# A GEGLU MLP on one core: w_down sums moved into the first pair of the following quad, and the owed gelu flushed one product later

## The chip, the cores and the metric

One core of a Trainium2 chip. The metric is the device time of one execution in microseconds (us), the median of several; all runs quoted here are fast, with a granted TensorE clock of 0.999 or 1.0. PE is TensorE, DVE VectorE, ACT ScalarE, POOL GpSimd, and SP the engine from which most transfers are issued.

## The reference

```python
x: (8, 1024, 1024) f32;  w_gate, w_up: (1024, 4096) f32;  w_down: (4096, 1024) f32
gate = x @ w_gate
up   = x @ w_up
gate = 0.5 * gate * (1 + tanh(sqrt(2 / pi) * (gate + 0.044715 * gate ** 3)))
return ((gate * up) @ w_down).astype(float32)
```

## The kernel before

The 8192 tokens are worked off in eight passes of 1024. Matrix products are made with fast (Strassen-like) schemes in f16: fewer matmuls, in exchange for sums of operands and results on DVE and ACT. Passes 0 to 2 use a scheme of 7 products instead of 8; in the gate/up stage of such a pass, one *pair* of column blocks of the weights takes 14 products (seven for gate, seven for up), and one product is four matmuls of 128x128 by 512. Two pairs are a *quad*: they share one load of raw weights.

Four names matter in a pair: P1 writes bank a, P5 bank b, then P6 adds onto bank a. Since P1's own result is needed later, ACT copies bank a to bank c ("copy 0" for gate, "copy 1" for up) before P6 may overwrite it.

```python
SEQ = [
    ("P1", 0), ("P1", 1), ("P5", 0), ("P6", 0), ("P6", 1), ("P5", 1), ("P7", 0),
    ("P7", 1), ("P2", 0), ("P4", 0), ("P4", 1), ("P2", 1), ("P3", 0), ("P3", 1),
]
AFTER1 = {                       # work put behind product k
    1: ["copy 0"], 2: ["copy 1"], 4: ["snap s2 0"], 5: ["snap s2 1"],
    ...
    13: ["add s2 0"], 14: ["add s2 1"],
}

def pair(p, i, extra, seq, after):
    ...
    for k, (name, w) in enumerate(seq, 1):
        product(name, w)
        if k == 1:
            flush()                          # gelu and product owed by the pair before
        for what in after.get(k, ()):
            do(what)                         # copy, snap: ACT; add, h: DVE
        for f in extra.get(k, ()):
            f()
    pending.extend([lambda: do("gelu s2"), lambda: do("prod s2")])
```

The last sums of a pair, "add s2" on DVE, end after its last product, so the gelu on them (ACT) and the product of gate and up (POOL) are owed to the next pair: `flush()` issues them there. The other names in `AFTER1`: a "snap" is ACT's copy of a finished bank to a tile in SBUF, an "add" is DVE's sum of bank b and such a tile, and an "h" is DVE's product of gate and up. ACT works through its own stream in the order in which the program issues it: in the lines of the prediction two copies whose input was ready stand behind a gelu before which ACT had been idle for 4.44 us.

In pass 0 the kernel also prepares w_down for the later down stages: in four groups it loads raw blocks of w_down (line 394, POOL's DMA queue, with a cast), makes four sums of them on DVE (lines 410, 412, 414, 416) and stores the results. `s0 + ds` is a running product number; 14 of them are a pair.

```python
for n in range(4):
    s0 = 28 * n + 59
    for ds, f, a in (
        (0, wd_load, (n, 0)), (2, wd_load, (n, 1)),
        (4, wd_load, (n, 2)), (6, wd_load, (n, 3)),
        (18, wd_sums, (0,)), (19, wd_sums, (1,)),
        (20, wd_sums, (2,)), (21, wd_sums, (3,)), (23, wd_store, (n,)),
    ):
        pr, k = divmod(s0 + ds - 1, 14)
        if pr == i:
            at(k + 1, f, *a)
```

In the first down stage, the transposing loads of x for the next pass and the loads of the stage's own w_down operands (chunks) share SP's queue:

```python
for v, name in enumerate(DSEQ):              # 7 products of 2 chunks kc each
    for nb in range(2):
        kc = 2 * v + nb
        for g in range(G):
            ... # 8 matmuls
            if nb == 0 and g == 0 and p + 1 < NPASS:
                ...
                if v == (3 - p if p < FAST - 1 else 0):
                    transpose_x(p + 1)       # four transposing DMAs
        load_d(p, kc + 6 if p else {0: 8, 6: 10, 8: 12}.get(kc, 14))
```

## Time and profile before

| | us |
|---|---|
| median of the first three runs | 2263.22 (2263.08 to 2264.55) |
| median of six runs | 2263.05 (2262.39 to 2264.55) |
| span of the profiled execution | 2261.1 |
| PE busy, PE idle by the page | 2247.4, 13.7 |
| gate/up stage of pass 0, 1, 2 | 183.75, 195.99, 194.86 |
| down stage of pass 0, 1, 2 | 97.69, 96.69, 96.70 |
| from the end of pass 2 to the end | 1366.9 |

The stages are differences of the first matmul starts of the stages in PE's timeline. The views and how to read them are shown with the prediction; the one thing to keep in mind is that a matmul's printed duration, 0.379 us, is not its share of time: in an unbroken run one starts every 0.216 us, as the prediction works out.

### The profile page before, as it was taken

Reading aid. Unit: us, or ns where it says so; the run is one execution under the profiler, and the core shown is the slowest. Engines: PE = TensorE matmul, PEld = TensorE weight load, DVE = VectorE, ACT = ScalarE, POOL = GpSimd, SP = SyncE. Lnnn points to the kernel's source line nnn. Section 1 sums busy time; section 2 is a strip of 40 time slices with the busy share of each in tenths; the row PEclk is TensorE's granted clock in tenths of the full one; section 3 lists DMA queues with packets and bytes.
Section 4 is the critical chain, followed back from the end, with each engine's and each line's share of the span. In section 5 each row is a group of like instructions: output and inputs, shape, how many; then the busy total and the mean of one; then the engine's idle time right before and its main releaser. Section 6 shows DMA issues by size and latency. Waiting matters only on the chain.

```text
span 2261.1 us, 42805 instructions
## 1 busy us (share of the span) xinstructions
PE 2247.4 (99%) x16634; PEld 1624.9 (72%) x16634; DVE 1565.3 (69%) x2190; ACT 954.6 (42%) x1866; POOL 686.0 (30%) x825
## 2 busy tenths in 40 slices
PE   9999999999999999999999999999999999999999
PEld 4444444444444445888888888888888888888888
DVE  6676468884488755877776677766776667866674
ACT  4444135651266522665126550355404553055520
POOL 1342013330133300555115450245402543044520
PEclk9999999999999999999999999999999999999999
DMA  9997969989999999999998999988999889888876
GB/s 241 191 207 187 274 189 236 253 258 284 266 223 243 270 311 346 332 336 379 302 336 275 318 301 317 326 273 321 310 320 318 282 313 325 312 314 277 283 288 225
DMA packets 308093, 642.46 MB, mean 284 GB/s; under 512 B 79088, under 2 KB 185328, under 8 KB 287344
## 3 DMA queue, kind: packets, MB, share of 16 engines
q1 hardware_dynamic: 253104, 566.57, 73.0%
q0 software_dynamic: 54784, 73.14, 19.2%
q8 instruction: 130, 2.13, 0.4%
q14 instruction: 75, 0.61, 0.1%
HBM read 574.36 MB, written 138.41 MB: 315 GB/s over the span
## 4 chain that ended last, share of the span: by engine, by line
PE 84%; DVE 3%; DMA 2%; SPq 0%; issue 0%; ACT 0%; DVEq 0%
PE ps L848 40%; PE ps L1099 20%; PE ps L626 14%; PE ps L991 10%; DMA wd_quads<-x_sums 1%; DVE ring L351 1%; DVE h_s L278 1%; DVE tmp L645 1%; DMA w_ops<-h_s 1%; SPq L255 0%; DMA ring<-wd_ops 0%; DVE x_sums L278 0%; DVE h_a L663 0%; ACT ps L642 0%; DVE h_a L923 0%
## 5 line engine op out<-in xcount | busy, mean ns | idle before, releaser
L848 PEld LDWEIGHTS <-ring 128*128 128x128 f16 x8320 | 814.1, 98 | 94.4
L825 POOL TENSOR_TENSOR h_a<-tmp 128x256 f16<-128x256 f32 x640 | 468.8, 752 | 839.8 <-ACT tmp L813 832.3
L848 PE MATMUL ps<-x_sums,ring 128*128 128x256 f16 x5760 | 655.8, 273 | 0.0
L810 DVE TENSOR_TENSOR tmp<-tmp,ps 128x512 f32<-128x512 f32 x640 | 414.4, 683 | 146.9 <-PE ps L848 100.4
L626 PEld LDWEIGHTS <-ring 128*128 128x128 f16 x2632 | 257.4, 98 | 317.0 <-issue 8.2
L795 ACT COPY tmp<-ps 128x512 f32<-128x512 f32 x520 | 304.0, 585 | 237.7 <-PE ps L848 163.9
L626 PE MATMUL ps<-x_sums,ring 128*128 128x512 f16 x1504 | 342.1, 379 | 4.1 <-DVE tmp L645 2.2
L813 ACT ACTIVATE tmp<-tmp 128x256 f32<-128x256 f32 x640 | 263.8, 418 | 173.3 <-DVE tmp L808 79.7
L848 PE MATMUL ps<-x_b,ring 128*128 128x256 f16 x2560 | 305.6, 273 | 0.0
L808 DVE TENSOR_TENSOR tmp<-ps,tmp 128x512 f32<-128x512 f32 x240 | 165.4, 689 | 145.2 <-ACT tmp L795 101.0
L652 POOL TENSOR_TENSOR h_a<-tmp 128x512 f16<-128x512 f32 x94 | 151.6, 1613 | 374.7 <-ACT tmp L650 259.8
L626 PE MATMUL ps<-x_b,ring 128*128 128x512 f16 x1128 | 259.2, 379 | 0.0
L1099 PEld LDWEIGHTS <-h_a 128*128 128x128 f16 x2240 | 219.1, 98 | 25.4
L991 PE MATMUL ps<-ring,h_a 128*128 128x512 f16 x1024 | 222.3, 379 | 0.8 <-DMA ring<-wd_ops 0.8
L1099 PE MATMUL ps<-ring,h_a 128*128 128x256 f16 x1920 | 216.1, 273 | 0.0
L991 PEld LDWEIGHTS <-h_a 128*128 128x128 f16 x1152 | 112.7, 98 | 137.0 <-DMA ring<-wd_ops 1.3
L645 DVE TENSOR_TENSOR tmp<-ps,tmp 128x512 f32<-128x512 f32 x188 | 127.2, 683 | 107.0 <-ACT tmp L637 104.1
L1156 ACT ACTIVATE tmp<-ps 128x512 f32<-128x512 f32 x60 | 35.3, 597 | 362.6 <-PE ps L1099 274.6
L1168 DVE SCALAR_TENSOR_TENSOR tmp<-ps,tmp 128x512 f32<-128x512 f32 x120 | 81.1, 690 | 97.5 <-PE ps L1099 66.7
L637 ACT COPY tmp<-ps 128x512 f32<-128x512 f32 x188 | 110.0, 586 | 87.2 <-PE ps L626 84.4
L351 DVE TENSOR_TENSOR ring<-ring 128x1024 f16<-128x1024 f16 x188 | 133.1, 722 | 8.7 <-DMA ring<-in_w_up_dram 4.5
L1099 PE MATMUL ps<-ring,x_sums 128*128 128x256 f16 x1120 | 126.4, 273 | 0.0
(102 smaller groups left out, 1536.6 us busy)
## 6 DMA issues: line engine op xcount, KB each, us to landing
ring<-w_ops SPq DMA_DIRECT2D x480, 512.0 KB, 4.8
ring<-wd_quads SPq DMA_DIRECT2D x110, 1024.0 KB, 6.8
ring<-wd_ops SPq DMA_DIRECT2D x35, 1024.0 KB, 8.0
out_dram<-tmp SPq DMA_DIRECT2D x128, 256.0 KB, 6.5
w_ops<-h_s SPq DMA_DIRECT2D x128, 256.0 KB, 7.0
ring<-in_w_gate_dram POOLq DMA_DIRECT2D x23, 1024.0 KB, 10.2
ring<-in_w_up_dram POOLq DMA_DIRECT2D x23, 1024.0 KB, 17.9
wd_quads<-x_sums SPq DMA_DIRECT2D x131, 128.0 KB, 6.5
```

The lines of the kernel that those rows point to most:

```text
L351: nc.vector.tensor_tensor(o, a, b, op)
L626: nc.tensor.matmul(ps(b, w), lhs[:, k], rhs[:, k, :], start=(first and k == 0), stop=(k == KH - 1), skip_group_check=True,)
L645: nc.vector.tensor_tensor(o, ps("b", w), o, ADD)
L652: nc.gpsimd.tensor_tensor(hq[TO[n]][:, i, :], tmp[:, t[n, 1]], tmp[:, t[n, 0]], MUL)
L795: nc.scalar.copy(tmp[:, t[o[1]]], ps_all[:, bank[o[2]]])
L808: nc.vector.tensor_tensor(d, b, a, SUB)
L810: nc.vector.tensor_tensor(d, a, b, ADD if o[4] == "add" else SUB)
L813: nc.scalar.activation(d, d, GELU, scale=GSC)
L825: nc.gpsimd.tensor_tensor(h, tmp[:, t[o[1]], MQ : 2 * MQ], g, MUL)
L848: nc.tensor.matmul(ps_all[:, bank[c], w * MQ : (w + 1) * MQ], lhs[:, w, k], rhs[:, k], start=(first and w == 0 and k == 0), stop=(k == KH ...
L991: nc.tensor.matmul(ps_all[:, bank[b, g]], lhs[:, j, g * P : (g + 1) * P], dc[:, n, :], start=(first and j == 0), stop=(j == NP - 1), skip_ ...
L1099: nc.tensor.matmul(ps_all[:, bank[c], m * MQ : (m + 1) * MQ], lhs[:, j, m * P : (m + 1) * P], rhs[:, j, :], start=(first and j == 0 and m ...
```

## The change

Two edits with one intent: to take away what PE waits for in the pairs of passes 0 to 2. The owed work goes behind both copies; the w_down sums leave the pair in which DVE waited for their loads and go into the pair after it, with loads that start 13 products later.

```diff
             product(name, w)
-            if k == 1:
-                flush()
             for what in after.get(k, ()):
                 do(what)
+            if k == 2:
+                flush()
             for f in extra.get(k, ()):
                 f()
 ...
-                    s0 = 28 * n + 59
+                    s0 = 28 * n + 72
                     for ds, f, a in (
                         (0, wd_load, (n, 0)), (2, wd_load, (n, 1)),
                         (4, wd_load, (n, 2)), (6, wd_load, (n, 3)),
-                        (18, wd_sums, (0,)), (19, wd_sums, (1,)),
-                        (20, wd_sums, (2,)), (21, wd_sums, (3,)), (23, wd_store, (n,)),
+                        (22, wd_sums, (0,)), (23, wd_sums, (1,)),
+                        (24, wd_sums, (2,)), (25, wd_sums, (3,)), (26, wd_store, (n,)),
                     ):
```

## The prediction

> **What bounds the kernel now.** I read the page first. Its first section says that there is little to win:
>
> ```profile
> PE 2247.4 (99%) x16634; PEld 1624.9 (72%) x16634; DVE 1565.3 (69%) x2190; ACT 954.6 (42%) x1866; POOL 686.0 (30%) x825
> ```
>
> The reader is to see that TensorE (PE) is busy for 2247.4 of 2261.1 us. Nothing of its own work is changed (the built programs have the same PE instructions in the same order), so only waits can be won: 13.7 us of visible idle time. Next, the waits of PE alone:
>
> ```profile
> PE ps L626 <- DVE tmp L645: 2.2, 7, 0.4
> PE ps L626 <- ACT ps L642: 1.9, 4, 0.5
> ...
> PE ps L991 <- DMA ring<-wd_ops: 0.8, 1, 0.8
> ```
>
> L626 is the matmul of the gate/up pairs in passes 0 to 2, which the change touches: eleven waits, 4.1 us. The other idle time is the start (4.5 us before 30 us), one DMA wait in the first down stage (0.8) and the tail after the last matmul (about 4.3); the sum is 13.7. None of those three is touched. The fast passes after 894 us show no wait.
>
> Where the eleven lie, I took from PE's timeline. One of them, in pass 0:
>
> ```profile
> 86.60 4.48 PE L626 MATMUL ps<-x_b,ring 128*128 128x512 f16 x20
> 90.92 1.03 PE L626 MATMUL ps<-x_sums,ring 128*128 128x512 f16 x4
> 92.34 4.48 PE L626 MATMUL ps<-x_sums,ring 128*128 128x512 f16 x20 [0.40 <-DVE tmp L645]
> ...
> 99.25 4.48 PE L626 MATMUL ps<-x_b,ring 128*128 128x512 f16 x20
> ```
>
> A product is four matmuls. Twenty take 4.48 us, of which the last matmul's own 0.379 us is pipeline, so one starts every (4.48-0.379)/19 = 0.216 us, a product takes 0.863 us and a pair of 14 products 12.08 us. The run of 20 is the last three products of a pair (P2, P3, P3) and the first two of the next (P1, P1), so a pair begins 12 matmuls into it, here at 89.19. Its third product is P5 (90.92); the fourth is P6, on the bank that P1 wrote. P6 should start 4 x 0.216 after 90.92, at 91.78; it starts at 92.34. **The loss is 0.56 us, though the profile calls 0.40 idle**: the printed end of a matmul lies 0.163 us (0.379-0.216) after the point where the next could have started. The starts of the runs agree: 86.60 to 99.25 is 12.65, against 12.08 for a pair without a wait.
>
> Why P6 waits is in the timeline of all engines:
>
> ```profile
> 86.33 1.27 POOL L652 TENSOR_TENSOR h_a<-tmp 128x512 f16<-128x512 f32 x1 [6.93 <-ACT tmp L650]
> 86.37 1.77 DVE L416 TENSOR_TENSOR h_s<-h_s 128x1024 f16<-128x1024 f16 x1
> ...
> 90.46 0.68 DVE L645 TENSOR_TENSOR tmp<-ps,tmp 128x512 f32<-128x512 f32 x1
> ...
> 91.17 0.63 ACT L650 ACTIVATE tmp<-tmp 128x512 f32<-128x512 f32 x1 [4.44 <-DVE tmp L645]
> ...
> 91.71 1.06 ACT L642 COPY ps<-ps 128x512 f32<-128x512 f32 x2
> ```
>
> The add "s2 0" (L645) of the previous pair ends late, at 91.14. The owed gelu (L650) waits for it, and the two copies of the P1 sums (L642) stand behind the gelu on ScalarE though their input was ready at about 91. P6 overwrites the bank that copy 0 reads, so it waits for that copy, which ends near 92.3. The profile names DVE since another add happens to end at 92.34; I take the copy as the releaser, because the program has P6 wait for ScalarE. A wait in pass 1 has the same form, with ScalarE named:
>
> ```profile
> 372.37 0.63 ACT L650 ACTIVATE tmp<-tmp 128x512 f32<-128x512 f32 x1 [4.38 <-DVE tmp L645]
> ...
> 372.90 1.06 ACT L642 COPY ps<-ps 128x512 f32<-128x512 f32 x2
> ...
> 373.53 2.75 PE L626 MATMUL ps<-x_sums,ring 128*128 128x512 f16 x12 [0.34 <-ACT ps L642]
> ```
>
> All eleven waits stand between P5 and P6, four in pass 0 in the pair after the w_down sums, four in pass 1, three in pass 2.
>
> **What the Trainium skill says.** "PSUM — Partial Sum Buffer", section "Engine vs sequencer instructions": the ScalarE, VectorE and GpSimd queues are strict FIFO. The trace agrees: copies whose input was ready stood behind a gelu that sat 4.44 us for an add. "SBUF — State Buffer", section "Who interferes with whom": a VectorE instruction with two SBUF inputs contends with a GpSimd instruction that reads SBUF. The trace agrees: the sum L416 started inside a GpSimd product and took 1.77 us, all four of its kind 1.767 or more, against 0.68 for L412. "DMA: Bandwidth & Descriptors", section "Anatomy of one DMA — SWDGE (gpsimd) path", has a fit of about 2.0 us plus bytes over 436 GB/s, which gives an estimate of 2.6 us for the 256 KB w_down loads; the trace has 9.1 to 12.3 from issue to landing behind other traffic, and I use the trace.
>
> **The change part by part.** *Flush one product later.* The owed gelu and its GpSimd product move behind both copies. Copy 0 then needs only P1's end (pair start + 0.86, some 0.1 to see it), and ends near +1.55; P6 is due at +2.59. Nothing late stands ahead of it, so each of the eleven waits should go. From the starts of the runs as above their costs are: pass 0, 4 x 0.56 = 2.25; pass 1, 0.50+0.69+0.36+0.69 = 2.24; pass 2, 0.35+0.70+0.36 = 1.41. **The sum is 5.9 us.** No instruction is added. What is delayed: the gelu now starts at +2.4 (after copy 1) and ends near +3.0. Next on ScalarE is the snap of s2, which cannot start before P6 ends at about +3.55. So it is free, except where another ScalarE operation of 1.06 us (L374) and one of 0.63 us stand there too: once in pass 2, by my count of the steps, snap would end 0.1 to 0.2 us after P7 wants it at +5.18. I give 0.2 us for this.
>
> *Sums into the next pair.* Their four loads move 13 products (11.2 us) later, the four sums 17 products. The first sum now waits 13.8 us in four waits for its loads, but that is idle time of VectorE at the start of a pair, where its next work comes only at 83.97 anyway; taking it away gives PE nothing directly. Before, the loads went out from 68.67 and VectorE came to the first sum at 78.0, 9.3 us later. Now they should go out some 4.5 us into a pair (behind the later GpSimd product) and the sum come some 9 us into the next: 12.1-4.5+9 = 16.6 us, enough for the longest, 12.3. Removing 0.68x3+1.77 = 3.8 us from one pair's VectorE and putting it into the next one's last five products does not shorten the chain: I reckon with the add s2 0 about 2 us into the following pair, as late as today. With copies ahead of the gelu that no longer matters. So: 0 us beside the flush.
>
> Sum: 2263.2 - 5.9 + 0.2 = 2257.5.
>
> **The rivals.** (1) *Only part goes*: if the sums are what made the adds late, and the order on ScalarE not, then only pass 0's 2.25 us go: 2261.0. Against it: passes 1 and 2 show the same chain without any such sum. (2) *VectorE becomes late enough to matter*: the bank that P5 takes is freed by the h product on VectorE. In the pairs with the moved sums that product should end near +11.5 to +11.8, and P5 is due at +13.8 on the same scale; for a stall the sums would have to come 2 us later than I think. Four such stalls of 0.5 us would leave 2259.5. (3) *A transfer*: weight loads now follow the w_down loads more closely. DMA is nearly full in pass 0 (0.92 to 1.17 busy between 40 and 180 us). But a weight load lands in 8.6 to 15.1 us and is needed some 22 after its issue; a delay of 4 us stays hidden. (4) *The DMA wait in the first down stage* (0.8) could grow or go with shifted traffic: about 1 us either way.
>
> **Range and chances.** The three runs before spread over 1.5 us. With that, rival 4 and half of rival 2: 2255.8 to 2260.2. Two per cent is 45 us, over three times all visible idle time; slower by that needs a fault that I do not see.
>
> **What would show it.** Right: no PE wait at L626 in any of the eleven places; every pair 12.08 us apart; PE's wait list left with the start and the L991 line; L642 ahead of L650 in each pair; no wait of L410 for its load; the add s2 0 still late in the pairs after the sums. Wrong: a PE wait for h (L663) or for the snap (L637), a longer L991 wait, or waits at L626 that survive, which would mean that the copy was not the releaser.

## The result, and the profile after

2256.48 us (median of six, 2255.86 to 2259.28) against 2263.05 (six runs on the same chips). The ratio is 0.9973, with a 95% interval of 0.996 to 0.9986: the mean time of the changed kernel's fast runs over that of the fast runs of before in the same rounds, so not quite the ratio of the medians. By the yardstick of 2% this is the same; the difference of 6.6 us is clear of the spread all the same, since none of these six runs of before is below 2262.39 and none of the changed kernel above 2259.28.

The line of the changed kernel's page that answers to the first one in the prediction:

```profile
PE 2246.1 (100%) x16634; PEld 1625.6 (72%) x16634; DVE 1561.7 (69%) x2190; ACT 956.1 (42%) x1866; POOL 679.3 (30%) x825
```

PE has the same instructions and 1.3 us less busy time in a span of 2254.4 us, 6.7 less: what went is mostly idle time (13.7 us before, 8.3 now). The waits of PE, whole list (what is waited for, us in total, times, longest):

```profile
PE ps L1219 <- DVE h_s L1222: 1.6, 1, 1.6
PE ps L1198 <- DVE x_b L305: 1.1, 2, 0.6
PE ps L1198 <- ACT ring L331: 0.6, 1, 0.6
PE ps L991 <- DMA ring<-wd_ops: 0.4, 1, 0.4
PE ps L303 <- DVE h_a L297: 0.2, 1, 0.2
```

All eleven waits at L626, the matmul of the pairs, are gone. What remains are the start (lines 303, 1198, 1219) and one transfer in the first down stage. PE's timeline over the first 320 us (start, duration, engine, line, operation, output and inputs, shape, count) at the place that the prediction shows:

```profile
86.58 4.48 PE L626 MATMUL ps<-x_b,ring 128*128 128x512 f16 x20
90.90 5.34 PE L626 MATMUL ps<-x_sums,ring 128*128 128x512 f16 x24
...
98.67 4.48 PE L626 MATMUL ps<-x_b,ring 128*128 128x512 f16 x20
```

P5, P6 and P7 are one unbroken run of 24, and the pairs are 98.67-86.58 = 12.09 us apart, where it had been 12.65. All engines at the next start of a pair, which begins twelve matmuls into the run of 98.67, at 101.26; the sums have moved into the pair before it:

```profile
101.59 0.68 DVE L645 TENSOR_TENSOR tmp<-ps,tmp 128x512 f32<-128x512 f32 x1
102.19 0.68 DVE L416 TENSOR_TENSOR h_s<-h_s 128x1024 f16<-128x1024 f16 x1
102.32 0.57 ACT L642 COPY ps<-ps 128x512 f32<-128x512 f32 x1 [3.52 <-PE ps L626]
...
103.24 0.57 ACT L642 COPY ps<-ps 128x512 f32<-128x512 f32 x1 [0.35 <-PE ps L626]
103.72 0.63 ACT L650 ACTIVATE tmp<-tmp 128x512 f32<-128x512 f32 x1
```

Copy 0 starts as soon as P1 is done ("<-PE ps L626": ACT waited for PE, not for DVE) and the gelu comes third. Two things differ from what the prediction says: the add s2 0 ends at 102.27, 1.0 us into the pair and not 2, and L416 takes 0.68 us and not 1.77.

Where the time went, stage by stage (us):

| stage | before | changed | difference |
|---|---|---|---|
| start, to the first L626 | 28.54 | 28.72 | +0.18 |
| gate/up, pass 0 | 183.75 | 181.32 | -2.43 |
| down, pass 0 | 97.69 | 97.29 | -0.40 |
| gate/up, pass 1 | 195.99 | 193.39 | -2.60 |
| gate/up, pass 2 | 194.86 | 193.39 | -1.47 |
| the rest | 1460.3 | 1460.3 | 0.0 |

The rest is both other down stages and the five fast passes. The sum is -6.7, the difference of the spans (2261.1-2254.4). Each column is one profile: the -0.40 is within what the down stage varies by, and in passes 1 and 2 a delay of 0.25 to 0.5 us comes and goes from profile to profile while the gelu is ahead of the copies (see the sums alone). The two stages of 193.39 are 896 matmuls at 0.2158 us each: at that rate nothing is left to win there without fewer matmuls.

### The profile page after: what moved, and what is told of

Read it like the earlier page. It is cut to its first block, busy times and chain, and to the rows that moved or that the text cites. A ratio compares the mean times of both kernels' runs of the same rounds, so it can differ in the third digit from the quotient of the medians.

```text
span 2254.4 us, 42805 instructions
## 1 busy us (share of the span) xinstructions
PE 2246.1 (100%) x16634; PEld 1625.6 (72%) x16634; DVE 1561.7 (69%) x2190; ACT 956.1 (42%) x1866; POOL 679.3 (30%) x825
## 3 DMA queue, kind: packets, MB, share of 16 engines
q0 software_dynamic: 54784, 73.14, 19.3%
## 4 chain that ended last, share of the span: by engine, by line
PE 87%; DMA 2%; SPq 0%; DVE 0%; issue 0%; DVEq 0%
PE ps L848 40%; PE ps L1099 20%; PE ps L626 17%; PE ps L991 10%; DMA wd_quads<-x_sums 1%; SPq L255 0%; DMA ring<-wd_ops 0%; DVE x_sums L452 0%; DVE h_a L923 0%; DVE tmp L1168 0%; DVE x_sums L278 0%; SPq L487 0%; DVEq L278 0%; SPq L535 0%
## 5 line engine op out<-in xcount | busy, mean ns | idle before, releaser
L626 PEld LDWEIGHTS <-ring 128*128 128x128 f16 x2632 | 257.5, 98 | 310.4
L626 PE MATMUL ps<-x_sums,ring 128*128 128x512 f16 x1504 | 339.8, 379 | 0.0
L626 PE MATMUL ps<-x_b,ring 128*128 128x512 f16 x1128 | 259.1, 379 | 0.0
L652 POOL TENSOR_TENSOR h_a<-tmp 128x512 f16<-128x512 f32 x94 | 144.5, 1537 | 374.8 <-ACT tmp L650 271.9
L991 PE MATMUL ps<-ring,h_a 128*128 128x512 f16 x1024 | 222.3, 379 | 0.4 <-DMA ring<-wd_ops 0.4
L991 PEld LDWEIGHTS <-h_a 128*128 128x128 f16 x1152 | 112.7, 98 | 136.6 <-DMA ring<-wd_ops 0.9
L645 DVE TENSOR_TENSOR tmp<-ps,tmp 128x512 f32<-128x512 f32 x188 | 127.2, 683 | 112.6 <-ACT tmp L637 111.1
L351 DVE TENSOR_TENSOR ring<-ring 128x1024 f16<-128x1024 f16 x188 | 138.7, 751 | 11.1 <-DMA ring<-in_w_up_dram 6.9
```

The lines of the kernel that those rows point to most:

```text
L351: nc.vector.tensor_tensor(o, a, b, op)
L626: nc.tensor.matmul(ps(b, w), lhs[:, k], rhs[:, k, :], start=(first and k == 0), stop=(k == KH - 1), skip_group_check=True,)
L645: nc.vector.tensor_tensor(o, ps("b", w), o, ADD)
L652: nc.gpsimd.tensor_tensor(hq[TO[n]][:, i, :], tmp[:, t[n, 1]], tmp[:, t[n, 0]], MUL)
L991: nc.tensor.matmul(ps_all[:, bank[b, g]], lhs[:, j, g * P : (g + 1) * P], dc[:, n, :], start=(first and j == 0), stop=(j == NP - 1), skip_ ...
```

## The experiments

Two theories of why the eleven waits went. The first: P6 waits for copy 0 alone, and copy 0 stood on ACT behind a gelu that waited for a late add; the order on ACT is the whole cause, and the moved sums add nothing. The second: DVE is what is late, and in pass 0 the sums had to move. Each run below was compared with before in five rounds on one chip.

| run | edit to | median us | gate/up 0, 1, 2 | down 0 | waits at L626 |
|---|---|---|---|---|---|
| flush alone | before | 2257.21 | 181.43, 193.39, 193.39 | 98.92 | 0 |
| sums alone | before | 2260.37 | 181.32, 195.49, 195.11 | 97.11 | 6 |
| gelu between the copies | before | 2256.58 | 181.31, 193.46, 193.47 | 97.29 | 0 |
| sums early | before | 2260.85 | 181.32, 195.48, 195.10 | 98.26 | 6 |
| load first | changed | 2255.66 | 181.32, 193.39, 193.38 | 96.69 | 0 |
| changed, again | none | 2256.43 | 181.40, 193.39, 193.39 | 97.46 | 0 |
| flush alone, load first | before | 2255.80 | 181.31, 193.38, 193.38 | 96.70 | 0 |
| load first, again | changed | 2255.85 | 181.31, 193.39, 193.39 | 96.69 | 0 |

Before, in the same rounds: 2262.99 for the first four, 2263.26 for the next two, 2262.60 for the last two. The stages are from the one profiled execution of each. All outputs are right.

### The flush alone

The kernel before with the first hunk of the diff and not the second.

> The kernel before with the flush alone moved behind the second copy; the w_down loads and sums stay where they were. Theory (the copy behind the late gelu is what holds P6; its order on ScalarE is the whole cause): all eleven PE waits at L626 go, PE's three gate/up stages take about 181.3, 193.4 and 193.4 us as in the changed kernel, time 6.0 to 6.7 us below before, within 0.7 us of the changed kernel. VectorE still waits about 13.8 us at L410 and still takes 1.77 us for L416, and the add s2 0 in the pairs of the sums is still about 1.9 us late: none of it costs PE anything. Rival (the moved sums are needed for pass 0): passes 1 and 2 gain 4.1 us, pass 0 nothing, four waits of 0.4 at L626 remain, time about 4.1 us below before.

Measured: 2257.21 us (2256.26 to 2258.30), ratio 0.9973, interval 0.9961 to 0.9986. The timeline of all engines where the prediction shows the wait of before; this pair starts at 87.11 + 12 x 0.216 = 89.70:

```profile
86.84 1.27 POOL L652 TENSOR_TENSOR h_a<-tmp 128x512 f16<-128x512 f32 x1 [4.78 <-ACT tmp L650]
86.89 1.77 DVE L416 TENSOR_TENSOR h_s<-h_s 128x1024 f16<-128x1024 f16 x1
...
90.77 0.57 ACT L642 COPY ps<-ps 128x512 f32<-128x512 f32 x1 [3.52 <-PE ps L626]
90.98 0.68 DVE L645 TENSOR_TENSOR tmp<-ps,tmp 128x512 f32<-128x512 f32 x1
91.43 1.89 PE L626 MATMUL ps<-x_sums,ring 128*128 128x512 f16 x8
...
92.17 0.63 ACT L650 ACTIVATE tmp<-tmp 128x512 f32<-128x512 f32 x1
```

The late DVE is all there: L416 at 1.77 us, the add s2 0 ending at 91.66, 1.96 us into the pair as before (91.14-89.19 = 1.95), and 16.2 us of waiting at L410 for the loads. But copy 0 starts before the add has even begun, and P5 and P6 are one run. All gate/up stages are within 0.12 us of their floor. The second theory falls for the change as made: with the flush moved, the sums need not move. This kernel's median is 0.7 us above the changed kernel's, in other rounds; in the profiled execution, the slowest of the five, most of the excess is in the down stage (98.92 us against 97.29). The last experiment comes back to it.

### The sums alone

The second hunk of the diff and not the first.

> The kernel before with the w_down loads and sums alone moved into the next pair; the owed gelu stays ahead of the copies. The prediction on record had this part at 0 us, with the add s2 0 about 2 us late as before: then four L626 waits of about 0.4 remain in pass 0 and the time is that of before. The theory after seeing the changed trace: there that add ends 1.0 us into the next pair (L416 takes 0.68 us instead of 1.77), so that even with the gelu ahead copy 0 ends at about +2.2 where P6 is due at +2.59: pass 0 loses its four waits (183.75 us becomes 181.3 to 181.6), passes 1 and 2 keep their seven (195.99 and 194.86 us), time about 2.3 us below before.

Measured: 2260.37 us (2259.98 to 2260.91), 2.6 us below before by the medians; ratio 0.9987, interval 0.9975 to 1.0000. The waits of PE at L626 that are left, six and all in passes 1 and 2:

```profile
PE ps L626 <- ACT ps L642: 1.6, 3, 0.5
...
PE ps L626 <- DVE tmp L645: 0.6, 3, 0.2
```

And the timeline of all engines in pass 0, at the pair that starts at 101.76:

```profile
102.10 0.68 DVE L645 TENSOR_TENSOR tmp<-ps,tmp 128x512 f32<-128x512 f32 x1
102.70 0.68 DVE L416 TENSOR_TENSOR h_s<-h_s 128x1024 f16<-128x1024 f16 x1
102.81 0.63 ACT L650 ACTIVATE tmp<-tmp 128x512 f32<-128x512 f32 x1 [3.50 <-DVE tmp L645]
...
103.34 1.06 ACT L642 COPY ps<-ps 128x512 f32<-128x512 f32 x2
```

The gelu still stands ahead of the copies, but the add is done at 102.78, 1.0 us into the pair; copy 0 ends at about 103.9 and P6 is due at 101.76+2.59 = 104.35. So this part alone is worth all of pass 0's 2.43 us. The prediction had it at 0 beside the flush; its working, with the add as late as before, leaves 0 for the part by itself too, and that was wrong. Either part wins pass 0's waits (2.43 us here, 2.32 with the flush alone), and together they win them once.

Seven waits had been expected to stay and six did. The missing one is in pass 1, where the program is that of before: there the add s2 0 of one pair ended 1.89 us into the next pair in the profile of before, and 0.82 here. In pass 2 another add was late in turn, by 0.25 us for PE (195.11 us against 194.86). The run with early sums shows the same. The same add ended at 1.68 us in the changed kernel's profile and at 0.36 in its repeat, so it moves between executions of one program; with one profile of before, nothing says that the sums moved it here, and why it moves is not known.

### The gelu between the two copies

```diff
-            if k == 1:
-                flush()
             for what in after.get(k, ()):
                 do(what)
+            if k == 1:
+                flush()
```

> The kernel before with the owed gelu between copy 0 and copy 1: copy 0 alone goes ahead of it. Theory (P6 of the first half waits for copy 0 and nothing else): gelu starts at the add's end, at about +2.0 to +2.1, copy 1 ends near +3.3, and the P6 that needs it is due at +3.45: no wait at L626, time as for the flush alone, 6.0 to 6.7 us below before. Rival (PE waits for the add on VectorE, as the profile names it in seven of eleven cases): the seven waits named DVE (0.56 us lost each in pass 0, 0.35 in passes 1 and 2, 3.3 us in sum) stay, and only some 2.6 us are won.

Measured: 2256.58 us (2256.37 to 2258.42), ratio 0.9973, interval 0.9960 to 0.9985. The timeline of all engines; the pair starts at 89.26:

```profile
90.32 0.57 ACT L642 COPY ps<-ps 128x512 f32<-128x512 f32 x1 [3.52 <-PE ps L626]
90.53 0.68 DVE L645 TENSOR_TENSOR tmp<-ps,tmp 128x512 f32<-128x512 f32 x1
90.98 2.32 PE L626 MATMUL ps<-x_sums,ring 128*128 128x512 f16 x10
91.24 0.63 ACT L650 ACTIVATE tmp<-tmp 128x512 f32<-128x512 f32 x1 [0.35 <-DVE tmp L645]
91.73 0.68 DVE L645 TENSOR_TENSOR tmp<-ps,tmp 128x512 f32<-128x512 f32 x1
91.78 0.58 ACT L642 COPY ps<-ps 128x512 f32<-128x512 f32 x1
```

The add s2 0 ends at 91.21, 1.95 us into the pair, and P6 runs through at its due time of 91.85 without a wait. The add that the profile of before names is the next one, s2 1, which ended as P6 began, 3.15 us into the pair. Here it ends 3.15 us into the pair again (91.73+0.68 = 92.41), 0.56 us after P6 has begun. So the profile's releaser in seven of the eleven waits of before, "DVE tmp L645", was a neighbour that ended at the same moment; what PE waited for was copy 0. Copy 1 ends at 92.36, and the P6 that needs it is due at 89.26 + 4 x 0.863 = 92.71, so the gelu fits between. In passes 1 and 2 that is nearly used up: the stages are 0.07 to 0.08 us above the floor.

### The sums early

```diff
-                        (18, wd_sums, (0,)), (19, wd_sums, (1,)),
-                        (20, wd_sums, (2,)), (21, wd_sums, (3,)), (23, wd_store, (n,)),
+                        (16, wd_sums, (0,)), (16, wd_sums, (1,)),
+                        (16, wd_sums, (2,)), (16, wd_sums, (3,)), (23, wd_store, (n,)),
```

> The kernel before with the four w_down sums one after the other ahead of the first add of the pair (loads and flush unchanged): they fall into the gap in which VectorE waited for its loads and then for its next input, 80.9 to 84.0 in the trace before. Theory (in pass 0 the add s2 0 is late because the last sums share a crowded end of the pair with h products, weight sums and adds, one of them, L416, at 1.77 us against a GpSimd product): L416 takes about 0.68 us, the add s2 0 ends about 1 us into the next pair or earlier, the four waits of pass 0 go, 2.3 us below before, seven waits remain. Rival (VectorE's sum of work in the pair is what makes it late, wherever the sums stand): waits of 0.4 remain, time of before.

Measured: 2260.85 us (2260.28 to 2262.41), 2.1 us below before by the medians; the interval of the ratio, 0.9977 to 1.0005, still includes 1. Pass 0 is at its floor of 181.32 us, six waits in passes 1 and 2 remain. DVE in the timeline of all engines; the next pair starts at 85.92 + 12 x 0.216 = 88.51:

```profile
82.68 0.68 DVE L416 TENSOR_TENSOR h_s<-h_s 128x1024 f16<-128x1024 f16 x1
...
83.29 0.69 DVE L645 TENSOR_TENSOR tmp<-ps,tmp 128x512 f32<-128x512 f32 x1
...
88.60 0.68 DVE L645 TENSOR_TENSOR tmp<-ps,tmp 128x512 f32<-128x512 f32 x1
```

The same four sums in the same pair, but ahead of POOL's product: none takes 1.77 us, and the add s2 0 ends 0.77 us into the next pair. It is not the amount of DVE work in the pair that made the add late; it is that the sums stood in its crowded second half, the last of them against POOL. How much of the lateness is L416's extra 1.09 us and how much the place of the other three, this run does not part. The profile of before gives an estimate: DVE runs there without a gap from L412 at 84.57 to the late add, so with L416 at 0.68 us the add would end 1.95-1.09 = 0.86 us into the pair, against 0.77 in this run and 0.77 to 0.78 after the two pairs of the same kind before that have no w_down sums. By that estimate most of the lateness is L416's extra. The down stage of pass 0 took 98.26 us in this profile, with a wait of 1.4 us at L991 that is put down to an add on DVE. It is the late load of the next experiment: the load of chunk 10 landed at 279.95 and PE went on at 280.00, as soon after it as in the six other profiles with this wait (0.04 to 0.05 us); that add happened to end at 279.96.

### The load ahead of the transposes

The first down stage is the one place after the start where the changed kernel still waits, and it differs from profile to profile. The timeline of SP in the kernel before (L255 the transposing loads of x, L535 the load of w_down chunk 10):

```profile
263.87 9.82 SPq L255 DMA_TRANSPOSE x_b<-x_half  x4
273.79 0.53 SPq L535 DMA_DIRECT2D ring<-wd_ops  x1
```

SP needed 9.82 us to issue four transposes, and the load stood behind them; it landed, at 282.30, when PE had been waiting for 0.8 us. The edit, on the changed kernel:

```diff
-                        if v == (3 - p if p < FAST - 1 else 0):
+                        if p and v == (3 - p if p < FAST - 1 else 0):
                             transpose_x(p + 1)
+                    if p == 0 and v == 3 and nb == 1 and g == 0:
+                        transpose_x(1)
```

> The changed kernel, with one further edit: in the first down stage the four transposing DMAs of x for the next pass go out one chunk later, so that the load of w_down operand chunk 10 stands ahead of them on the SP queue. In the traces so far that load was issued behind some 10 us of transposes and PE waited for it (L991: 0.8 before, 0.4 changed, 2.1 with the flush alone), and the stage took 97.11 to 98.92 us where the same stage of passes 1 and 2 takes 96.69. Theory (the rest of the difference between kernels and runs is this wait): no wait at L991, stage 96.7 to 96.9 us, time 0.4 to 1.2 us below the changed kernel of the same rounds. Rival (the load is slow since DMA is full, not late): the wait stays or moves to another chunk or to the transposes' users, and the time is the same.

> The changed kernel unmodified, once more, beside the run above and on its chip: 2256.5 us within 0.7, gate/up stages 181.3, 193.4, 193.4 us, first down stage between 97.1 and 98.9 us. It is the measure of what run to run moves, and what the kernel above is compared with.

Measured in the same rounds: 2255.66 us (2255.40 to 2255.85) with the edit, 2256.43 (2255.34 to 2257.41) without. SP's timeline without the edit and with it:

```profile
261.37 10.12 SPq L255 DMA_TRANSPOSE x_b<-x_half  x4
271.59 0.59 SPq L535 DMA_DIRECT2D ring<-wd_ops  x1
```

```profile
261.37 0.40 SPq L535 DMA_DIRECT2D ring<-wd_ops  x1
261.83 13.54 SPq L255 DMA_TRANSPOSE x_b<-x_half  x4
```

The load goes out 10 us earlier in its stage, there is no wait at L991, and the stage takes 96.69 us, as in passes 1 and 2. The medians differ by 0.77 us, as the stages of the two profiles do (97.46-96.69); the ranges overlap by one run, so the gain in time is small and rests on the trace. With it the spread shrinks from 2.1 to 0.45 us. The rival, that the transfer is slow rather than late, falls: from issue to landing the load took 7.3 us with the edit and 8.3 without, and the 10 us are in its issue.

### Is anything left for the moved sums?

The same edit on the flush alone, beside a repeat.

> The flush alone (w_down loads and sums where they were before) with the load of chunk 10 ahead of the transposes. In the profiled runs so far the first down stage took 97.1 to 97.5 us where the sums had been moved and 97.3 to 98.9 where they had not, so the moved sums might be worth something there. Theory (once the load goes out in time the place of the sums is worth nothing): stage 96.7 us, no L991 wait, time equal within 0.4 us to the run below, about 2255.7. Rival (the old place of the sums and loads costs the down stage something by itself): stage above 96.9, time 0.5 to 1.5 us above the run below.

> The changed kernel with the load of chunk 10 ahead of the transposes, again, in the same rounds as the run above: 2255.7 us within 0.4, no L991 wait, first down stage 96.7 us. It repeats the best version so far and is what the run above is compared with.

Measured: 2255.80 us (2255.56 to 2255.95) with the sums at their old place, 2255.85 (2255.41 to 2256.02) with the sums moved. The first down stage takes 96.7 us in both. So once the flush is moved and the load goes out in time, the place of the sums is worth nothing that five rounds show. These two and the first run with the load ahead are the best versions: some 7 us below before and 0.6 to 0.8 below the changed kernel. Whether the old place of the w_down loads makes the late load later (98.92 and 98.26 us in two profiles, 97.69 and 97.29 in two others, against 97.11 to 97.46 with loads and sums moved) stays open; with the load first it does not matter.

## Why the prediction was right, point by point

- **Only waits can be won: right.** PE's busy time is 2246.1 us against 2247.4 and its idle time 8.3 against 13.7, and nothing past 894 us changed.
- **All eleven waits at L626 go: right**, and for the reason given. The flush alone takes all of them, and the run with the gelu between the copies shows that copy 0, not the add, was the releaser in those that were named DVE.
- **5.9 us: a little small.** The three stages lost 2.43+2.60+1.47 = 6.50 us. The sum had 2.25, 2.24 and 1.41, because it counted only the places that the profile marks as idle. A matmul that starts up to 0.163 us late shows no idle time at all; against the floor of 193.39 us there were 0.36 us of unmarked delays in pass 1, five of them by the starts (0.02 to 0.18 us; the longest left 0.016 us idle, which the timeline does not mark). The step of converting 0.40 idle into 0.56 lost was right: pairs that were 12.65 us apart are now 12.09.
- **0.2 us for a late snap in pass 2: did not occur.** The stage is at its floor. It is a term that was argued from order and durations and not seen.
- **The sums: 0 beside the flush, right; the working, wrong.** The prediction held that the add would be "as late as today", 2 us. It measured 1.0 us, and at their new place no sum runs for 1.77 us against POOL: L416 is at 0.68, and the longest is an L412 at 0.92 in the pair shown. That this is the reason is argued; the new pair also has its weight sums early, not in its second half. The total was saved by the two parts winning the same wait, which is luck. By itself the part is worth 2.43 us in pass 0, not 0.
- **The loads: right.** L410 has no wait. It was overcautious: the loads now land in 5.6 us by the median (3.5 to 8.9), 13 products later than before and so further from the weight loads that go ahead of them on the same queue; that this is the reason is argued, not tested.
- **Rivals.** Rival 1 held the late sums against the order on ACT. In pass 0 both are true: the sums make the add late, and either cure is enough. A stall on DVE's h product did not come. Weight loads did get slower in pass 0, up to 19.3 us from 15.1, but within the margin: PE shows no wait for them. The flush alone, with the w_down loads at their old place, had 18.5, so their new place is not the only reason. The wait of the first down stage changed its stage by -0.40 us in this pair of profiles and by -0.23 in the repeat; with the flush alone it was +1.23, the about 1 us that the range allowed for.

By the two profiles, the predicted 2257.5 against 2256.48 is thus 0.6 us of unmarked delays, 0.4 us of the down stage and 0.2 us of a stall that did not come, less 0.18 us at the start. The middle term is what the down stage happened to do in these two executions.

## What to carry to other kernels

On an engine that works in order, put first what another engine waits for, and what itself waits for something late after it; here that one move took every wait in the pairs, and the work being late no longer mattered there. When two edits aim at one wait, test each alone: both can be enough, as in pass 0 here, and then the sum of their gains is an illusion. On a nearly full PE, compare the starts of equal runs of matmuls, since the idle time that the profile prints leaves out what the pipeline hides.

## What the Trainium skill lacked or had wrong

- "Perfetto Trace Analysis", section "Per-instruction lifecycle: what the profiler-reported window actually captures", says that a TensorE end time is estimated and not observed. The trace fits that (0.379 us printed on each, one start every 0.216), and the page could say what follows for gaps: 0.40 us of idle time after a matmul was 0.56 us lost (pairs 12.65 us apart against 12.09), and delays below 0.163 us leave no idle time at all.
- "SBUF — State Buffer", section "Who interferes with whom", has the contention of a VectorE operation on two SBUF inputs with a GpSimd operation that reads SBUF, and calls the shared ports an exclusive lock, but has no durations for such a pair. Here a sum of 128x1024 f16 took 1.77 us instead of 0.68 when it started 0.04 us into a GpSimd product of 1.27 us, and 0.92 when it started 1.15 us into one of 1.52. All 38 w_down sums that started inside a product, in nine profiles, ended 0.55 us after its end, as if each had waited it out.
- "DMA: Bandwidth & Descriptors", section "Anatomy of one DMA — SWDGE (gpsimd) path": its fit gives an estimate of 2.6 us for the 256 KB that such a load writes (3.2 for the 512 KB of f32 that it reads); in this kernel's traffic the loads took 9.1 to 12.3 us, and 3.5 to 8.9 when issued 13 products later. The fit is for one DMA; it does not give the time of loads issued amid this traffic.
- The same page, section "DMA Transpose (X-bar)", has no figure for how long transposing DMAs hold the issuing queue (the page's only sequencer times for them are cycles for small tiles, in a table about trn3). Four of them took 9.8 to 10.9 us of SP's time in the seven profiles where the load stood behind them, and 13.5 to 13.9 in the three where it went first.
